# Two sides of one memory: a pool of matmul operands moved from the upper to the lower end of the partitions, the stage pools from the lower to the upper

## The chip, the core and the metric

One core of a Trainium2 chip runs the whole program. The metric is the device time of one execution in microseconds (us), as the median of three runs. The profile is of one further execution of the same program.

## What is computed

Three transformer blocks over 512 tokens of width 1024, all in float32: forgetting attention (`fox`), dilated attention in three groups (`dil`), each followed by a gated embedding layer (`ple`), and a second block with a short convolution, sparse attention in three branches and a gated feed-forward layer. Cut to what matters here, the reference is a chain of projections:

```python
h = h + fox_mixer(rms_norm(h, fox_norm[j]), fox_w_in[j], fox_b_f[j], fox_w_out[j])
h = h + (p[i] @ ple_w_up[i]) * jax.nn.sigmoid(h @ ple_w_gate[i])      # after each mixer
h = h + dilated_mixer(rms_norm(h, dil_norm[j]), dil_w_in[j], dil_w_out[j])
...
proj = h @ w_in[l]
mix = gm[..., :D_MODEL] * (y_a @ w_a_out[l]) + gm[..., D_MODEL:] * (y_b @ w_b_out[l])
x = x + mix @ w_o[l]
gu = h @ w_ffn_in[l]
x = x + (jax.nn.silu(g) * gu[..., D_FF:]) @ w_ffn_out[l]
```

## The kernel before

Every projection is a product of a weight and an activation that are each split into a high and a low fp32r part, so one product takes three matmuls: high by high, high by low, low by high (`mm3`, L144 to L146). The activation of a layer stands in SBUF as eight pairs of tiles of 128 partitions by 512 tokens, 2048 bytes in each partition: `a0h, a0l, ... a7l` (pool `x`, called A) and `b0h, b0l, ... b7l` (pool `xb`, called B). A layer reads one of the two and writes the other:

- `fo` (8 units) reads B; gate 0 (8) reads A; `dq`, `dk`, `dz` (56) and `dv` (24) read B; `do` (8) reads A; gate 1 (8) reads B.
- In the second block most units read A; `wa` and `wb` (4 each) read one half of B; `wo` (8) and the feed-forward's `fg` and `fu` (44) read half their tiles from A and half from B; `f2` (22) takes its tiles in turn, four from B and four from A.

A unit is one weight of 128 by 1024 floats: a 512 KB DMA, a copy on ACT for the high part (`whi`, L74), a subtraction on DVE for the low part (`wlo`, L85), and 24 matmuls of 512 columns. In most units (`t_unit`, `k_outer`, `t_two`) the weight is the stationary operand and A or B moves; in `n_chunk` (L248 to L250: `v`, `dv`, `nq`, `nkv`) the weight moves and 128 columns of A or B are stationary. For two of the three groups of `dv` those 128 columns are every fourth one.

The order of the work is written out by hand; nothing schedules it. Units are woven with the steps of the attention of the stage. Waits follow from the tiles: a tile that is placed where an earlier one lay waits for the last access to the earlier one.

SBUF is handed out from both ends of a partition. From the lower end: `const`, `small`, the weights (`w`), A (`x`), and on top of them the pool of the stage that runs (`fox`, `ple0`, `dil`, `ple1`, `b2` with `b2t`, `b2a`, `b2g`, `wo`, `ffn`), which is opened when the stage begins and closed at its end. From the upper end: B alone (`open_b`, `side="right"`). While `b2t` lives, B is closed. The start of some tiles, in bytes within a partition, and what is left over multiples of 64:

| tiles | before | left over 64 | changed | left over 64 |
|---|---|---|---|---|
| A: `a0h` (16 tiles, 2048 apart) | 78016 | 0 | 77824 | 0 |
| B: `b0h` (16 tiles, 2048 apart) | 196576 | 32 | 110592 | 0 |
| weights: `whi`, `wlo` (first of five) | 37056, 57536 | 0 | 36864, 57344 | 0 |
| `fox`: `v_sb` | 110784 | 0 | 147360 | 32 |
| `fox`: `qs`, `kk`, `pr`, `pt` (first) | 148192, 156384, 164576, 177120 | 32 | 184768, 192960, 201152, 213696 | 0 |
| `ple0`, `ple1`: `p0h` | 147648, 147648 | 0 | 212672, 211104 | 0, 32 |
| `ple0`: `hA` | 110784 | 0 | 175808 | 0 |
| `dil`: `dqk`, `dpt` | 140480, 175552 | 0 | 185792, 220864 | 0 |
| `b2`: `q00`, `k00h` | 110784, 127168 | 0 | 178944, 195328 | 0 |
| `b2t`: `qn`, `kd` | 160864, 212800 | 32, 0 | 122912, 174848 | 32, 0 |
| `b2a`: `pr`, `pt` | 160864, 173536 | 32 | 144768, 157440 | 0 |
| `small`: `nacc` | 18432 | 0 | 18336 | 32 |

Of the kernel before, what the change touches and what calls it, by code (L numbers as in the profile page):

```python
# [9 lines left out]
F32 = mybir.dt.float32  # L10
# [6 lines left out]
P = 128  # L17
S = 512
D = 1024
KT = 8  # L20
# [86 lines left out]
def run(chunks):  # L107
    for c in chunks:
        if c:
            c()  # L110
# [17 lines left out]
class Net:  # L128
# [19 lines left out]
    def t_unit(self, tag, pair, kts, evac, m=P, tag_ps="acc"):  # L148
# [7 lines left out]
        for u, lst in enumerate(kts):  # L156
            for c0 in range(0, len(lst), 4):
                sub = lst[c0 : c0 + 4]

                def chunk(u=u, sub=sub, c0=c0, first=(c0 == 0), pos=pos):  # L160
                    if pos == 0:
                        st["acc"] = self.bank(tag_ps)
                    if first:
                        st["w"] = self.w.pop(tag)
                    self.w.pump()
                    wh, wl = st["w"]
                    for j, (c, k) in enumerate(sub):
                        self.mm3(st["acc"][:m], wh[:, c : c + m], wl[:, c : c + m], *pair[k],
                                 pos + j == 0, pos + j == total - 1)
                    if c0 + len(sub) == len(kts[u]):  # L170
                        self.w.n_done += 1
                    if pos + len(sub) == total:
                        self.soft_end()
                        run([evac(st["acc"])])

                chunks.append(chunk)
                pos += len(sub)
# [5 lines left out]
    def k_outer(self, tags, evacs, pair):  # L183

        st = {}

        def chunk(k):
            if k == 0:
                st["w"] = [self.w.pop(t) for t in tags]
                st["a"] = [self.acc() for _ in tags]  # L190
            self.w.pump()
            for (wh, wl), a in zip(st["w"], st["a"]):
                self.mm3(a, wh[:, k * P : (k + 1) * P], wl[:, k * P : (k + 1) * P], *pair[k],
                         k == 0, k == KT - 1)
            if k == KT - 1:
                self.w.n_done += len(tags)

        def evac():
            rest = [e(a) for e, a in zip(evacs, st["a"])]
            self.w.finish()  # L200
            run(rest)

        return [lambda k=k: chunk(k) for k in range(KT)] + [evac]
# [57 lines left out]
    def rsqrt(self, y, t, a):  # L261
        run(self.rsqrt_steps(y, t, a))
# [42 lines left out]

    def norm_factors(self, ss, n):

        r = self.small.tile([P, 3, 8], F32, name="rr", tag="rr", bufs=1)
        t, a, y = r[:, 0, :n], r[:, 1, :n], r[:, 2, :n]
        self.nc.vector.tensor_scalar(t, ss[:, :n], 1.0 / D, EPS, ALU.mult, ALU.add)  # L310
        self.rsqrt(y, t, a)
        return y
# [75 lines left out]
    def run(self):  # L388
        ctx, tc, nc, t = self.ctx, self.tc, self.nc, self.t
        pool = lambda name, bufs=1, **k: ctx.enter_context(tc.tile_pool(name=name, bufs=bufs, **k))  # L390
        c = pool("const")
        self.small = pool("small")
        wpool = pool("w")
        xp = pool("x")
        self.ps = pool("ps", space=bass.MemoryType.PSUM)
        self.w = Weights(tc, wpool, self.plan(), raw_ahead=7, ahead=4, raw_bufs=3, bufs=5)

        self.ident = c.tile([P, P], F32, name="ident")
        self.ones = c.tile([P, 1], F32, name="ones")
        self.sel = c.tile([P, 32], F32, name="sel")  # L400
        nc.vector.memset(self.ones, 1.0)
        self.gains = c.tile([P, 6, KT], F32, name="gains")
        nc.sync.dma_start(self.gains[:, 0:5, :], t["gains"])
        self.pos = c.tile([P, 4], I32, name="pos")
        self.sin, self.cos = (c.tile([P, 4, 32], F32, name=n) for n in ("sin", "cos"))
        self.inv = self.sin[:, 0, :]

        self.A = self.eight(xp, "a")
        self.open_b()
        self.h_dram = tc.dram_tile([D, S], F32, name="h_dram")  # L410
        self.m1_dram = tc.dram_tile([D, S], F32, name="m1_dram")
        self.x2_dram = tc.dram_tile([D, S], F32, name="x2_dram")
        self.fox()
        self.ple(0)
        self.dil()
        if self.stop == "dil":
            self.ples.close()
            return
        self.ple(1)
        self.block2()  # L420
        if self.stop == "b2":
            return
        self.ffn()
        self.bs.close()
# [3 lines left out]

    def open_b(self):
        self.bs = ExitStack()  # L430
        bp = self.bs.enter_context(self.tc.tile_pool(name="xb", bufs=1, side="right", reuse_waits="tile"))
        self.B = self.eight(bp, "b")


    def fox(self):
        tc, nc, t = self.tc, self.nc, self.t
        es = ExitStack()
        at = es.enter_context(tc.tile_pool(name="fox", bufs=1, reuse_waits="tile"))
        A, B = self.A, self.B
        v_sb = at.tile([P, 4, D], F32, name="v_sb")  # L440
        xs = v_sb.rearrange("p a (b s) -> p (a b) s", b=2)
# [261 lines left out]
    def ple_open(self, res_src, i):  # L703
        nc = self.nc
        self.ples = ExitStack()
        self.pl = self.ples.enter_context(self.tc.tile_pool(name=f"ple{i}", bufs=1, reuse_waits="tile"))
        self.hA = self.pl.tile([P, KT, S], F32, name="hA")
        self.u = self.pl.tile([P, KT, S], F32, name="u")
        for n in range(KT):
            nc.sync.dma_start(self.hA[:, n, :], self.rows(res_src, n))  # L710
        pr = self.pl.tile([P, 2, S], F32, name="p_raw")
        self.pp = [tuple(self.pl.tile([P, S], F32R, name=f"p{k}{x}") for x in "hl") for k in range(2)]
        for k in range(2):
            nc.sync.dma_start(pr[:, k, :], self.t["pT"][i, k * P : (k + 1) * P, :])
        self.pr = pr
# [49 lines left out]
    def dil(self):  # L765
        tc, nc, t = self.tc, self.nc, self.t
        es = ExitStack()
        at = es.enter_context(tc.tile_pool(name="dil", bufs=1, reuse_waits="tile"))
        A, B = self.A, self.B
        dist = self.load(at, "dist", t["dil_dist"], 1, (P, 1280))  # L770
        v = [at.tile([P, 4, S], F32, name=f"v{g}") for g in range(3)]
# [173 lines left out]
    def block2(self):  # L945
        tc, nc, t = self.tc, self.nc, self.t
        self.bs.close()
        es, es2 = ExitStack(), ExitStack()
        at = es.enter_context(tc.tile_pool(name="b2", bufs=1, reuse_waits="tile"))
        tmp = es2.enter_context(tc.tile_pool(name="b2t", bufs=1, reuse_waits="tile"))  # L950
        A = self.A
        v = nc.vector
        R = {}
# [7 lines left out]
        mwin = self.load(at, "mwin", t["mwin"], 1)  # L961
        mcmp = self.load(at, "mcmp", t["mcmp"], 1, (P, 132))
        cw = self.load(at, "cw", t["cw"], 1, (P, 12))
        rope = []
        self.ng = self.load(at, "ng", t["b_ng"].broadcast_to([P, 256]), 1, (P, 256))
        qn = tmp.tile([P, 4, S], F32, name="qn")
# [345 lines left out]
        es2.close()  # L1312
        self.open_b()
        es3 = ExitStack()
        aa = es3.enter_context(tc.tile_pool(name="b2a", bufs=1, reuse_waits="tile"))
        rest = conv[self.PRE :]
        for i in range(4):
            rest += T("g1", ev_gm(2 * i, 0)) + T("g1", ev_gm(2 * i + 1, 0))
# [5 lines left out]
        run(rest[: self.SK])  # L1324
        weave(rest[self.SK :], [lambda j=j: slot(j) for j in range(48 + LAG + 2)])
        es3.close()
        bb = es.enter_context(tc.tile_pool(name="b2g", bufs=1, reuse_waits="tile"))
        for n in range(3):
            fetch_m1(n)
        run(g2[0] + g2[1] + wb[0] + g2[2] + g2[3] + wb[1] + g2[4] + g2[5] + g2[6] + g2[7] + wb[2] + wb[3])  # L1330
        es.close()
        wo = ExitStack()
        wp = wo.enter_context(tc.tile_pool(name="wo", bufs=1, reuse_waits="tile"))
        hr = {}
        self.norm_begin()

# [47 lines left out]
    def ffn(self):  # L1384
        tc, nc, t = self.tc, self.nc, self.t
        v = nc.vector
        es = ExitStack()
        at = es.enter_context(tc.tile_pool(name="ffn", bufs=1, reuse_waits="tile"))
        cw = self.load(at, "fcw", t["fcw"], 1, (P, 88))
        act = at.tile([P, 22, S], F32, name="act")  # L1390
        cv = [at.tile([P, 514], F32, name=f"fcv{i}") for i in range(3)]
# [47 lines left out]
        for k in range(22):  # L1439
# [3 lines left out]
            if k < 22 - last:  # L1443
                wh, wl = self.w.pop("f2")
                for n in range(KT):
                    if n == 4:
                        self.w.pump()
                    c = n * P
# [5 lines left out]
        for n in range(KT):  # L1454
            for k, (wh, wl) in held:
                c = n * P
# [118 lines left out]
```

## Time and profile before

| | us |
|---|---|
| runs | 1758.46, 1757.23, 1757.28 (median 1757.28) |
| the profiled execution's own time | 1755.62 |
| its span, first to last instruction | 1753.8 |
| PE busy in the span | 1737.2 |
| DVE, ACT, POOL busy | 967.3, 673.4, 111.5 |

The span is 1.8 us shorter than its execution's own time, and that time is 1.7 us below the median of the runs. In the rows further down, a line such as L144 is a line of the kernel before; PE is the matrix engine, PEld its loading of the stationary operand, which runs beside it. A matmul's duration goes from its start to its end; since matmuls overlap in the engine, the step from one start to the next is what a matmul costs.

### The profile page before, as it was taken

How to read it: one execution, taken by the hardware profiler on the slowest of the kernel's cores; microseconds unless marked ns; L12 is line 12 of the kernel's file. 1: busy time of each engine (PE TensorE's matmuls, PEld its weight loads, DVE VectorE, ACT ScalarE, POOL GpSimd, SP SyncE). 2: the span in 40 equal slices, each digit the busy share in tenths (PEclk: the TensorE clock that was granted, in tenths of full speed). 3: DMA queues.
4: the chain of work that ended last, by engine and by line, in shares of the span. 5: the costliest groups of instructions: out<-in, count | busy, mean ns of one | idle time of the engine just before them, and what ended most of it. 6: DMA issues, size and time to landing. Idle time of an engine off the chain costs nothing.

```text
span 1753.8 us, 21614 instructions
## 1 busy us (share of the span) xinstructions
PE 1737.2 (99%) x8512; PEld 1400.6 (80%) x8512; DVE 967.3 (55%) x1692; ACT 673.4 (38%) x1146; POOL 111.5 (6%) x88
## 2 busy tenths in 40 slices
PE   8999999999999999999999999999999999999999
PEld 6777777888977779977778786777788888888887
DVE  6477774542354443354455777776544675566332
ACT  5466653422222222222245445455432333333220
POOL 2000000100000000000000411000000122111000
PEclk9999999999999999999999999999999999999999
DMA  5422224323222223222233422112233433223421
GB/s 165 143 87 96 84 68 144 125 103 113 84 85 70 75 72 96 84 84 70 75 107 121 158 95 72 58 51 92 87 130 118 151 121 96 93 91 100 139 96 59
DMA packets 57351, 173.75 MB, mean 99 GB/s; under 512 B 7441, under 2 KB 7953, under 8 KB 57249
## 3 DMA queue, kind: packets, MB, share of 16 engines
q1 hardware_dynamic: 57248, 172.36, 29.8%
q8 instruction: 67, 1.10, 0.3%
q14 instruction: 36, 0.29, 0.1%
HBM read 161.82 MB, written 10.52 MB: 98 GB/s over the span
## 4 chain that ended last, share of the span: by engine, by line
PE 93%; DVE 4%; ACT 2%; POOL 1%; issue 0%; DMA 0%; SPq 0%; ACTq 0%; DVEq 0%
PE acc L144 21%; PE acc L146 20%; PE acc L145 20%; PE acc L248 3%; PE acc L250 3%; PE acc L249 3%; PE o L698 2%; PE t L690 2%; PE s L144 1%; PE s L146 1%; PE s L145 1%; PE s L248 1%; PE s L250 1%; PE s L249 1%; PE s L677 1%; PE s L676 1%
## 5 line engine op out<-in xcount | busy, mean ns | idle before, releaser
L85 DVE TENSOR_TENSOR wlo<-wraw,whi 128x1024 fp32r<-128x1024 f32 x267 | 347.9, 1309 | 139.1 <-ACT whi L74 138.9
L74 ACT ACTIVATE whi<-wraw 128x1024 fp32r<-128x1024 f32 x267 | 279.2, 1050 | 166.3 <-PE acc L145 71.4
L626 ACT ACTIVATE pr<-pr,st 128x512 f32<-128x512 f32 (+3 forms) x160 | 93.6, 586 | 155.7 <-DVE st L823 83.9
L291 POOL TENSOR_TENSOR nacc<-nacc,sq 128x512 f32<-128x512 f32 x35 | 47.9, 1378 | 1198.2 <-ACT sq L290 1197.8
L779 DVE TENSOR_TENSOR dqk<-acc,nacc 128x512 f32<-128x512 f32 x24 | 26.1, 1100 | 63.7 <-PE s L812 59.0
L693 ACT ACTIVATE pt<-t 128x512 f32<-128x512 f32 (+3 forms) x128 | 51.0, 424 | 18.8 <-PE t L690 17.8
L1410 ACT ACTIVATE fy<-fcv,fcw 128x512 f32<-128x512 f32 x22 | 18.0, 816 | 102.6 <-DVE fcv L1405 102.6
L1423 POOL TENSOR_TENSOR act<-fs,fu 128x512 f32<-128x512 f32 x22 | 43.8, 1991 | 195.6 <-DVE fu L1422 178.1
L690 PE MATMUL t<-ident,pr 128*128 128x128 f32 x320 | 51.0, 273 | 2.2 <-ACT pt L693 1.2
L690 PEld LDWEIGHTS t<-ident,pr 128*128 128x128 f32 x320 | 39.7, 139 | 14.4 <-DVE pr L638 1.6
L144 PE MATMUL acc<-a0h,whi 128*128 128x512 f32 x112 | 48.5, 433 | 1.2 <-DVE zh L609 1.2
L822 DVE SCALAR_TENSOR_TENSOR pr<-dist,s 128x128 f32<-128x128 f32 (+1 forms) x96 | 24.9, 315 | 44.3 <-PE s L816 44.3
L144 PE MATMUL acc<-b4h,whi 128*128 128x512 f32 x113 | 46.5, 411 | 0.0
L635 DVE RECIPROCAL st<-st 128x1 f32<-128x1 f32 x160 | 24.1, 158 | 40.5 <-ACT pr L626 40.5
L144 PE MATMUL acc<-b7h,whi 128*128 128x512 f32 x113 | 45.5, 403 | 0.0
L145 PE MATMUL acc<-b7l,whi 128*128 128x512 f32 x113 | 45.3, 401 | 0.0
L146 PE MATMUL acc<-b7h,wlo 128*128 128x512 f32 x113 | 45.2, 400 | 0.0
L144 PE MATMUL acc<-b5h,whi 128*128 128x512 f32 x113 | 44.9, 397 | 0.0
L145 PE MATMUL acc<-b6l,whi 128*128 128x512 f32 x113 | 44.7, 396 | 0.0
L146 PE MATMUL acc<-b4h,wlo 128*128 128x512 f32 x113 | 44.7, 396 | 0.0
L146 PE MATMUL acc<-b5h,wlo 128*128 128x512 f32 x113 | 44.7, 395 | 0.0
L144 PE MATMUL acc<-b6h,whi 128*128 128x512 f32 x113 | 44.6, 395 | 0.0
(1107 smaller groups left out, 4694.6 us busy)
## 6 DMA issues: line engine op xcount, KB each, us to landing
wraw<-in_dil_q SPq DMA_DIRECT2D x24, 512.0 KB, 3.3
wraw<-in_dil_k SPq DMA_DIRECT2D x24, 512.0 KB, 3.3
wraw<-in_dil_v SPq DMA_DIRECT2D x24, 512.0 KB, 3.3
wraw<-in_f_g SPq DMA_DIRECT2D x22, 512.0 KB, 3.5
wraw<-in_f_u SPq DMA_DIRECT2D x22, 512.0 KB, 3.6
wraw<-in_f_o SPq DMA_DIRECT2D x22, 512.0 KB, 3.5
wraw<-in_gate SPq DMA_DIRECT2D x16, 512.0 KB, 3.3
wraw<-in_b_gm SPq DMA_DIRECT2D x16, 512.0 KB, 3.5
```

What stands on the lines that cost most here:

```text
L74: nc.scalar.activation(hi, t, AF.Copy)
L85: self.nc.vector.tensor_tensor(lo, t, hi.bitcast(F32), ALU.subtract)
L144: mm(acc, wh, xh, start=start, stop=False)
L145: mm(acc, wh, xl, start=False, stop=False)
L146: mm(acc, wl, xh, start=False, stop=stop)
L248: self.nc.tensor.matmul(a, sh, mh, start=(k == 0), stop=False)
L249: self.nc.tensor.matmul(a, sh, ml, start=False, stop=False)
L250: self.nc.tensor.matmul(a, sl, mh, start=False, stop=(k == KT - 1))
L291: nc.gpsimd.tensor_tensor(self.nacc[i], self.nacc[i], sq, ALU.add)
L626: self.nc.scalar.activation(pr, pr, AF.Exp, scale=-1.0, bias=st[:, 0:1], accum_out=st[:, 1:2])
L690: nc.tensor.transpose(tp[:, c : c + P], pr[:, c0 + kb * P : c0 + (kb + 1) * P], self.ident)
L693: nc.scalar.activation(pts[h][:, self.KOFF[kb] : self.KOFF[kb] + b - a], tp[:, a:b], AF.Copy)
```

## The change

The stage pools take the upper end of the partitions and B the lower, right above A. `gains` and `rr` move from `const` and `small` to a new pool `edge` at the very top, and two unused tiles (`align`, 96 bytes in each partition; `align2`, 32 bytes) fill up `const` and `b2`. No instruction is added, taken away or put elsewhere in any engine's order; what differs is where tiles lie, and with it which earlier tile some instructions wait for.

```diff
@@ norm_factors
-        r = self.small.tile([P, 3, 8], F32, name="rr", tag="rr", bufs=1)
+        r = self.edge.tile([P, 3, 8], F32, name="rr", tag="rr", bufs=1)
@@ run
         xp = pool("x")
+        self.edge = pool("edge", side="right")
...
-        self.gains = c.tile([P, 6, KT], F32, name="gains")
+        c.tile([P, 24], F32, name="align")
+        self.gains = self.edge.tile([P, 6, KT], F32, name="gains")
@@ open_b
-        bp = self.bs.enter_context(self.tc.tile_pool(name="xb", bufs=1, side="right", reuse_waits="tile"))
+        bp = self.bs.enter_context(self.tc.tile_pool(name="xb", bufs=1, reuse_waits="tile"))
@@ fox; the same in ple_open, dil, block2 (b2, b2t, b2a, b2g, wo) and ffn
-        at = es.enter_context(tc.tile_pool(name="fox", bufs=1, reuse_waits="tile"))
+        at = es.enter_context(tc.tile_pool(name="fox", bufs=1, side="right", reuse_waits="tile"))
@@ block2
         cw = self.load(at, "cw", t["cw"], 1, (P, 12))
+        at.tile([P, 8], F32, name="align2")
```

One place where waits differ is the opening of `ple0` behind `fox`. SyncE's queue there before (`hA` is the residual, `p_raw` the layer's embedding, `wraw` a raw weight; in brackets the engines and DMA queues that a row waits for):

```order
L44 DMA wraw<-in_fox_o 128x1024 [waits DMAHW6_49,DMAHW2_49,DVE_49]
L710 DMA hA<-in_xT 128x512 [waits PE_49]
L710 DMA hA<-in_xT 128x512 [waits DMAHW4_49]
L710 DMA hA<-in_xT 128x512 x2
L710 DMA hA<-in_xT 128x512 [waits DMAHW7_49]
L710 DMA hA<-in_xT 128x512 [waits DMAHW0_49]
L710 DMA hA<-in_xT 128x512 [waits DMAHW1_49]
L710 DMA hA<-in_xT 128x512 [waits DMAHW2_49]
L714 DMA p_raw<-in_pT 128x512 [waits DMAHW3_49,DVE_49]
L714 DMA p_raw<-in_pT 128x512 [waits DMAHW4_49]
L44 DMA wraw<-in_up 128x1024 [waits DMAHW5_49,DVE_49]
```

and with the change (two lines further down in the file):

```order
L44 DMA wraw<-in_fox_o 128x1024 [waits DMAHW6_49,DMAHW2_49,DVE_49]
L712 DMA hA<-in_xT 128x512 [waits DVE_49,PE_49]
L712 DMA hA<-in_xT 128x512 [waits DMAHW4_49]
L712 DMA hA<-in_xT 128x512 x2
L712 DMA hA<-in_xT 128x512 [waits DMAHW7_49]
L712 DMA hA<-in_xT 128x512 [waits DMAHW0_49]
L712 DMA hA<-in_xT 128x512 [waits DMAHW1_49]
L712 DMA hA<-in_xT 128x512 [waits DMAHW2_49]
L716 DMA p_raw<-in_pT 128x512 [waits DMAHW3_49,PE_49]
L716 DMA p_raw<-in_pT 128x512 [waits DMAHW4_49]
L44 DMA wraw<-in_up 128x1024 [waits DMAHW5_49,DVE_49]
```

The first load of `hA` now lies where `fox` kept small operands that DVE reads last, and waits for DVE beside PE; before, it lay on `v_sb`, which PE reads last. At the opening of `dil`, in the same way, the load of `dist` no longer waits for the writes of `hA` to DRAM, and the first `dqk` on DVE does.

## Rows read from the trace of the kernel before

**Rows 1.** The page's parts 1 and 4: busy time of the engines, and the chain of work that ended last.

```profile
PE 1737.2 (99%) x8512; PEld 1400.6 (80%) x8512; DVE 967.3 (55%) x1692; ACT 673.4 (38%) x1146; POOL 111.5 (6%) x88
...
PE 93%; DVE 4%; ACT 2%; POOL 1%; issue 0%; DMA 0%; SPq 0%; ACTq 0%; DVEq 0%
```

**Rows 2.** Busy time by stretch: for PE, PEld, DVE, ACT and POOL the us and the instructions, then TensorE's granted clock as a share of full speed, the DMA share and GB/s. The last stretch is the start of `dil`.

```profile
1500.00:1600.00 100.00, 100.00 (x433) 81.02 (x432) 64.51 (x70) 34.77 (x43) 16.08 (x9) 1.00 0.29 91
322.00:362.00 40.00, 40.00 (x177) 33.04 (x177) 26.50 (x30) 20.74 (x31) 7.79 (x6) 1.00 0.40 138
375.90:379.40 3.50, 3.50 (x9) 2.73 (x10) 1.84 (x11) 1.06 (x1) 0.00 (x0) 0.52 0.00 0
```

**Rows 3.** ACT's rows of gate 0, which reads A, in order of time: start, duration, then the instruction and what it waited for. One `th` follows the end of each unit of 24 matmuls.

```profile
320.66 0.60 ACT L748 ACTIVATE th<-acc 128x512 f32<-128x512 f32 x1 [3.89 <-PE acc L146]
326.10 0.60 ACT L748 ACTIVATE th<-acc 128x512 f32<-128x512 f32 x1 [1.16 <-PE acc L146]
...
358.74 0.60 ACT L748 ACTIVATE th<-acc 128x512 f32<-128x512 f32 x1 [1.16 <-PE acc L146]
```

**Rows 4.** The same of gate 1, which reads B.

```profile
951.75 0.60 ACT L748 ACTIVATE th<-acc 128x512 f32<-128x512 f32 x1 [0.93 <-PE acc L146]
957.35 0.60 ACT L748 ACTIVATE th<-acc 128x512 f32<-128x512 f32 x1 [0.71 <-PE acc L146]
962.95 0.60 ACT L748 ACTIVATE th<-acc 128x512 f32<-128x512 f32 x1 [0.70 <-PE acc L146]
968.55 0.60 ACT L748 ACTIVATE th<-acc 128x512 f32<-128x512 f32 x1
974.89 0.58 ACT L748 ACTIVATE th<-acc 128x512 f32<-128x512 f32 x1
```

**Rows 5.** PE's rows of one stretch of the feed-forward layer, in order of time: start, duration, matmul. One unit is 12 matmuls on A and 12 on B.

```profile
1500.21 0.40 PE L144 MATMUL acc<-a0h,whi 128*128 128x512 f32 x1
...
1501.83 0.39 PE L145 MATMUL acc<-a2l,whi 128*128 128x512 f32 x1
...
1502.74 0.39 PE L146 MATMUL acc<-a3h,wlo 128*128 128x512 f32 x1
1502.96 0.40 PE L144 MATMUL acc<-b4h,whi 128*128 128x512 f32 x1
...
1505.77 0.40 PE L144 MATMUL acc<-a0h,whi 128*128 128x512 f32 x1
```

**Rows 6.** Instructions by tile: duration in ns (least, median, most), first and last start in us. The first two have the tile moving in a layer's product, the others (with PEld, the load) stationary in `dv` (B) and in the two projections on A.

```profile
L144 PE MATMUL acc<-p0h,whi x16: 389/389/392, 304.1 to 944.6; 128*128 128x512 f32 x16
...
L144 PE MATMUL acc<-b5h,whi x113: 393/397/502, 269.7 to 1626.0; 128*128 128x512 f32 x113
...
L249 PE MATMUL acc<-wlo,b0h x18: 396/397/403, 397.6 to 708.7; 128*128 128x512 f32 x18
...
L249 PE MATMUL acc<-wlo,b1h x18: 392/399/409, 398.3 to 709.4; 128*128 128x512 f32 x18
...
L249 PE MATMUL acc<-wlo,a1h x9: 389/389/389, 56.9 to 1031.9; 128*128 128x512 f32 x9
```

**Rows 7.** DVE in the feed-forward layer, in order of time: the first evacuation of each pair of units.

```profile
1500.41 0.69 DVE L1405 TENSOR_TENSOR fcv<-acc,rb 128x512 f32<-128x512 f32 x1 [3.28 <-PE acc L146]
...
1511.53 0.69 DVE L1405 TENSOR_TENSOR fcv<-acc,rb 128x512 f32<-128x512 f32 x1 [3.28 <-PE acc L146]
```

**Rows 8.** DVE at the program's end, in order of time: an evacuation after each 15 matmuls of `f2` (9 on B, 6 on A).

```profile
1746.69 0.69 DVE L1458 TENSOR_TENSOR fr<-fr,acc 128x512 f32<-128x512 f32 x1 [2.80 <-PE acc L146]
1750.17 0.69 DVE L1458 TENSOR_TENSOR fr<-fr,acc 128x512 f32<-128x512 f32 x1 [2.79 <-PE acc L146]
```

**Rows 9.** PE at two places of the second block's scores, in order of time: matmuls of 512, 384 and 128 columns on a moving operand that starts at a multiple of 64 bytes.

```profile
1087.34 0.39 PE L676 MATMUL s<-k00h,q 128*128 128x512 f32 x1
1087.57 0.39 PE L677 MATMUL s<-k00l,q 128*128 128x512 f32 x1
...
1090.52 0.33 PE L676 MATMUL s<-k00h,q 128*128 128x384 f32 x1
1090.69 0.34 PE L677 MATMUL s<-k00l,q 128*128 128x384 f32 x1
1090.86 0.22 PE L676 MATMUL s<-k00h,q 128*128 128x128 f32 x1
1090.92 0.27 PE L677 MATMUL s<-k00l,q 128*128 128x128 f32 x1
```

**Rows 10.** The chain of work that ended last, in gate 1, in order of time: start, us, what (one turn of a loop through ACT and DVE).

```profile
967.67 0.96 ACT whi L74
968.66 2.15 DVE wlo L85
970.81 0.61 DVE th L749
971.45 0.70 DVE hA L750
972.17 0.72 ACT a3h L330
972.90 1.14 ACT sq L290 x2
974.04 0.96 ACT whi L74
```

**Rows 11.** The end of `fox` and the opening of `ple0`, in order of time; with the issue of a DMA on SyncE's queue (SPq) the duration is that of issuing.

```profile
269.82 4.38 SPq L710 DMA_DIRECT2D hA<-in_xT  x8
269.83 0.69 DVE L550 TENSOR_TENSOR zh<-o,zs 128x512 f32<-128x512 f32 x1 [7.81 <-PE o L698]
...
271.22 0.69 DVE L328 TENSOR_TENSOR b7l<-zh,b7h 128x512 fp32r<-128x512 f32 x1 [0.70 <-ACT b7h L327]
...
274.92 0.69 DVE L718 TENSOR_TENSOR hA<-hA,acc 128x512 f32<-128x512 f32 x1 [3.01 <-PE acc L146]
```

**Rows 12.** The page's part 6: DMA issues, count, KB each, median us to landing.

```profile
wraw<-in_dil_q SPq DMA_DIRECT2D x24, 512.0 KB, 3.3
...
hA<-in_xT SPq DMA_DIRECT2D x8, 256.0 KB, 4.0
```

**Rows 13.** Stationary loads of two tiles of `b2t`, by tile: duration in ns (least, median, most), first and last start in us.

```profile
L1064 PEld LDWEIGHTS t<-ident,kd x8: 138/140/142, 1068.1 to 1077.9; 128*128 128x128 f32 x8
...
L1054 PEld LDWEIGHTS t<-ident,qn x16: 137/139/143, 1049.4 to 1074.0; 128*128 128x128 f32 x16
```

More of the change, by code (lines that the diff above doesn't have):

```diff
@@ L705, in ple_open @@
         self.ples = ExitStack()
-        self.pl = self.ples.enter_context(self.tc.tile_pool(name=f"ple{i}", bufs=1, reuse_waits="tile"))
+        self.pl = self.ples.enter_context(self.tc.tile_pool(name=f"ple{i}", bufs=1, side="right", reuse_waits="tile"))
         self.hA = self.pl.tile([P, KT, S], F32, name="hA")
@@ L767, in dil @@
         es = ExitStack()
-        at = es.enter_context(tc.tile_pool(name="dil", bufs=1, reuse_waits="tile"))
+        at = es.enter_context(tc.tile_pool(name="dil", bufs=1, side="right", reuse_waits="tile"))
         A, B = self.A, self.B
@@ L948, in block2 @@
         es, es2 = ExitStack(), ExitStack()
-        at = es.enter_context(tc.tile_pool(name="b2", bufs=1, reuse_waits="tile"))
-        tmp = es2.enter_context(tc.tile_pool(name="b2t", bufs=1, reuse_waits="tile"))
+        at = es.enter_context(tc.tile_pool(name="b2", bufs=1, side="right", reuse_waits="tile"))
+        tmp = es2.enter_context(tc.tile_pool(name="b2t", bufs=1, side="right", reuse_waits="tile"))
         A = self.A
@@ L1314, in block2 @@
         es3 = ExitStack()
-        aa = es3.enter_context(tc.tile_pool(name="b2a", bufs=1, reuse_waits="tile"))
+        aa = es3.enter_context(tc.tile_pool(name="b2a", bufs=1, side="right", reuse_waits="tile"))
         rest = conv[self.PRE :]
@@ L1326, in block2 @@
         es3.close()
-        bb = es.enter_context(tc.tile_pool(name="b2g", bufs=1, reuse_waits="tile"))
+        bb = es.enter_context(tc.tile_pool(name="b2g", bufs=1, side="right", reuse_waits="tile"))
         for n in range(3):
@@ L1332, in block2 @@
         wo = ExitStack()
-        wp = wo.enter_context(tc.tile_pool(name="wo", bufs=1, reuse_waits="tile"))
+        wp = wo.enter_context(tc.tile_pool(name="wo", bufs=1, side="right", reuse_waits="tile"))
         hr = {}
@@ L1387, in ffn @@
         es = ExitStack()
-        at = es.enter_context(tc.tile_pool(name="ffn", bufs=1, reuse_waits="tile"))
+        at = es.enter_context(tc.tile_pool(name="ffn", bufs=1, side="right", reuse_waits="tile"))
         cw = self.load(at, "fcw", t["fcw"], 1, (P, 88))
```

## The prediction, made before the change was run

> **What bounds the kernel now.** I read the page's busy times and its chain first: PE is busy for 1737.2 of 1753.8 us and holds 93% of the chain [rows 1], DVE is the next at 55%. [...] So what a matmul costs from one start to the next is nearly all of the time, and a change that moves no instruction can only act through that step, or through waits.
>
> Next I compared that step between A and B. Gate 0 and gate 1 run the same code, eight units of 24 matmuls of 512 columns with the weight stationary; gate 0 moves A, gate 1 moves B. After gate 0's units `th` comes every 5.44 us (seven units from 320.66 to 358.74 [rows 3]), that is 226.7 ns a matmul. In gate 1 the first three steps are 5.60 us [rows 4], 233.3 ns a matmul. In both, `th` follows PE directly. The durations agree: 389 ns for `p0h`, which like A starts at a multiple of 64 bytes, and 397 for `b5h`, which starts 32 past one [rows 6]. Inside one unit of the feed-forward layer, with the same weight and the same PSUM tile, the step changes with the operand: the last five on A take 1.13 us (1501.83 to 1502.96, 226 ns each), the twelve on B 2.81 us (1502.96 to 1505.77, 234 ns each) [rows 5]. After B the first seven on A take 1.62 us (1500.21 to 1501.83, 231 ns) [rows 5], so a return from B to A costs some 35 ns more. A unit of both therefore takes 5.56 us (two take 11.12 from 1500.41 to 1511.53 [rows 7]) where one of A alone takes 5.44.
>
> What sets B apart in the table of tile starts is its 32 bytes over a multiple of 64 and its place above 196576. On a multiple of 64 the step goes with the columns alone: 0.23 us for 512, 0.17 for 384, 0.06 for 128 [rows 9], all near 0.444 ns a column. So no start cost per instruction is left there, and the 6.7 ns of B are something added per instruction. I take the offset as its cause.
>
> **The change part by part.** With the change B starts at a multiple of 64, as A and the weights still do. The counts are units from the list of layers, 24 matmuls each, at 24 x 6.67 ns = 0.16 us.
> - Units wholly on B, bound by PE: `fo` 8, `dil`'s `dq`, `dk`, `dz` 56, `wa` and `wb` 8, and two of gate 1: 74 x 0.16 = **11.8 us**. Gate 1's other six count nothing: from the third on a loop of ACT and DVE (`whi`, `wlo` 2.15 us, `th`, `hA`, `a3h`, two squares) takes 6.37 us a turn (967.67 to 974.04 [rows 10]), `th` then comes 6.34 us apart [rows 4], and PE waits for it.
> - Units half on B: `wo` 8, `fg` and `fu` 44: 52 x (5.56 - 5.44) = **6.2 us**.
> - `f2`: nine blocks of 24 on B before the last five are held back, 1.4 us; then eight outputs of 15 matmuls, 3.48 us apart [rows 8] against 15 x 0.2267 = 3.40, another 0.7: **2.1 us**.
> - `dv` has B stationary: 24 units. The 8 in plain order have 397 to 399 ns against 389 on A [rows 6] and I give them the same 0.16: **1.3 us**. The 16 that take every fourth column reach 409 [rows 6]; the stride can cost something of its own. Bounds: nothing, and the whole difference of about 10 ns (399 to 389) x 384 = 3.8 us; I take the 6.67 ns that the other B operands show, the nearest row: **2.6 us**.
> - Tiles that lose their multiple of 64: `ple1`'s `p` pairs, 48 matmuls x 6.67 ns = **-0.3 us**. `v_sb` loses it as the stationary operand of 128 matmuls while `pt`, which moves there, gains it; bounds -0.9 and +0.9 us, taken 0. `pr`, `qs` and `kk` gain it too: no row prices them alone, 0 to +1 us, taken 0. `nacc` is read by PE some 50 times for a norm: under 0.4 us, taken 0.
> - Waits at the openings. `hA`'s first load is issued at 269.82 now, waiting for PE [rows 11]. With the change it waits for DVE, `zh` ending at 270.52 or at the latest `b7l` at 271.91 [rows 11]: 0.7 to 2.1 us later. Behind it on SyncE's queue stand the other `hA` rows, `p_raw` and the weights of `up`. The first sum on `hA` starts at 274.92 [rows 11], a load takes 4.0 us to land [rows 12], so DVE may start up to 1 us late; but PE goes on into the units of n = 3 and needs the first PSUM tile back only 5.6 us later, which covers it. Were that cover gone, PE would lose the 2.1 us. The other openings I cost at nothing for the same reason: the loads are issued a unit or more ahead of use. Bounds 0 and 2.1 us.
> [...]
>
> Sum: 11.8 + 6.2 + 2.1 + 1.3 + 2.6 - 0.3 = **23.7 us less**. The profiled execution of 1755.62 us would be 1731.9 and its span 1730.1; its time is 1.7 us below the median of the runs, 1757.28, which becomes **1733.6**.
>
> [...]
>
> **The rivals.**
> - *The upper end is slow, not the offset.* B is also what lies highest, and no row has a full-rate operand up there on a multiple of 64. Then B still gains 23.7 us, but the stage operands that now lie above 196576 pay: by the code's loops 160 + 128 on `fox`'s `pr` and `pt`, 64 on its `kk`, 128 on `b2`'s `k`, in `dil` 120 on `pr`, 176 on `dpt` and half of 576 on `dqk`, 96 on the `p` pairs, in all 1160 matmuls x 6.67 ns = 7.7 us: 1757.3 - 23.7 + 7.7 = **1741.3**. Against it: `kd` at 212800, a multiple of 64, loads in 140 ns, and `qn` at 160864, 32 over, in 139 [rows 13], so height alone shows nothing there, if only for a stationary tile at half rate. Chance 0.07.
> - *The address is not the cause*, so nothing changes: **1757.3**. For it stands only that two layers differ in more than address; against it the switch inside one unit [rows 5]. Chance 0.05. [...]
> - *Slower: the openings wait.* Seven stages begin with loads (`ple0`, `dil`, `ple1`, `b2`, `b2g`, `wo`, `ffn`), and at the upper end their first tiles now lie on the previous stage's last-used ones. If each opening exposed one load to landing, 4.0 us [rows 12], that is 28 us: 1757.3 - 23.7 + 28 = **1761.6**. It decides from 23.7 + 3.5 = 27.2 us, 3.9 us at every one of the seven. Against it: the one place looked at in detail moves by 2.1 us at most, and some waits get shorter, as that of `dist`. Chance 0.04.
>
> **How the numbers follow.** The forecast has 0.84. Its own range: low if the strided `dv` gives all of its 3.8 us and `pr`, `pt` and the clock bring up to 2.5 more, 1730; high if strided `dv` gives nothing, an opening loses 2.1 and `v_sb` 0.9, 1739. To hold 8 in 10 I go from 1729.5 to 1741.5, which takes in the first rival. A measurement of this kernel can tell about 0.2%, 3.5 us. Faster by more: forecast and first rival, 0.91. Within it: 0.05. Slower: 0.04.
>
> **What the new profile would show.** Gate 1's first steps of `th` at 5.44 us instead of 5.60, its later ones still near 6.37; `b5h` at 389 ns; a pair of feed-forward units 10.88 us apart; the last outputs 3.40 us apart. The strided `dv` matmuls decide between 0 and 3.8 us. If `b` rows drop but `k00h`, `dpt` or `pt` rows get longer, the first rival holds. If `b` rows stay at 397, the second. New idle time of PE ended by a DMA at a stage's start would be the third.

## The result and the profile after

| | before | changed |
|---|---|---|
| runs, us | 1755.37, 1757.23, 1757.28, 1758.46 | 1738.31, 1740.25, 1740.27, 1740.29 |
| median | 1757.26 | 1740.26 |
| profiled execution, its span | 1755.62, 1753.8 | 1738.31, 1736.5 |

The ratio is 0.9903, 95% interval 0.9891 to 0.9916: 17.0 us less on the medians, 17.3 between the two profiled executions. The forecast was 1733.6 us with a range of 1729.5 to 1741.5: the sign and the range held, the sum of 23.7 us was 6 to 7 too large, and, as the experiments show, the cause was misnamed.

The page's parts 1 and 4 of the changed kernel, against [rows 1]: PE lost 18.5 us of busy time, and no other engine's changed by more than 1.0.

```profile
PE 1718.7 (99%) x8512; PEld 1401.6 (81%) x8512; DVE 967.3 (56%) x1692; ACT 672.8 (39%) x1146; POOL 111.0 (6%) x88
...
PE 92%; DVE 4%; ACT 2%; POOL 1%; issue 0%; DMA 0%; SPq 0%; ACTq 0%; DVEq 0%
```

ACT's `th` rows of gate 0 (first and last of eight) and gate 1, in order of time: start, duration, instruction, what it waited for.

```profile
320.50 0.60 ACT L750 ACTIVATE th<-acc 128x512 f32<-128x512 f32 x1 [3.92 <-PE acc L146]
...
358.58 0.60 ACT L750 ACTIVATE th<-acc 128x512 f32<-128x512 f32 x1 [1.16 <-PE acc L146]
...
942.47 0.60 ACT L750 ACTIVATE th<-acc 128x512 f32<-128x512 f32 x1 [0.81 <-PE acc L146]
947.91 0.60 ACT L750 ACTIVATE th<-acc 128x512 f32<-128x512 f32 x1 [0.55 <-PE acc L146]
953.35 0.60 ACT L750 ACTIVATE th<-acc 128x512 f32<-128x512 f32 x1 [0.54 <-PE acc L146]
959.09 0.57 ACT L750 ACTIVATE th<-acc 128x512 f32<-128x512 f32 x1
965.45 0.57 ACT L750 ACTIVATE th<-acc 128x512 f32<-128x512 f32 x1
```

Gate 0 stays at 5.44 us a unit [rows 3]. Gate 1 on B, 5.60 us before [rows 4], now also takes 5.44; a turn of 5.74 follows, and from 959.09 on ACT and DVE set 6.36 us a turn, as before.

PE in the feed-forward layer, in order of time (start, duration, matmul), to be held against [rows 5]:

```profile
1485.23 0.39 PE L144 MATMUL acc<-b4h,whi 128*128 128x512 f32 x1
...
1487.95 0.39 PE L144 MATMUL acc<-a0h,whi 128*128 128x512 f32 x1
...
1489.54 0.39 PE L145 MATMUL acc<-a2l,whi 128*128 128x512 f32 x1
```

Twelve on B take 2.72 us (226.7 ns each; 234 before), and the seven on A after them 1.59 (227; 231 before). DVE's first evacuation of each pair of units, against [rows 7], and the last two outputs of `f2`, against [rows 8]:

```profile
1488.15 0.69 DVE L1408 TENSOR_TENSOR fcv<-acc,rb 128x512 f32<-128x512 f32 x1 [3.03 <-PE acc L146]
...
1499.04 0.69 DVE L1408 TENSOR_TENSOR fcv<-acc,rb 128x512 f32<-128x512 f32 x1 [3.03 <-PE acc L146]
1509.91 0.69 DVE L1408 TENSOR_TENSOR fcv<-acc,rb 128x512 f32<-128x512 f32 x1 [3.03 <-PE acc L146]
...
1729.55 0.69 DVE L1461 TENSOR_TENSOR fr<-fr,acc 128x512 f32<-128x512 f32 x1 [2.71 <-PE acc L146]
1732.95 0.69 DVE L1461 TENSOR_TENSOR fr<-fr,acc 128x512 f32<-128x512 f32 x1 [2.71 <-PE acc L146]
```

10.88 us a pair and 3.40 an output, as the prediction said. Instructions by tile (least, median, most ns), against [rows 6]:

```profile
L144 PE MATMUL acc<-b5h,whi x113: 389/389/499, 270.2 to 1611.0; 128*128 128x512 f32 x113
...
L144 PE MATMUL acc<-p0h,whi x16: 392/394/400, 303.6 to 935.4; 128*128 128x512 f32 x16
...
L249 PEld LDWEIGHTS acc<-wlo,b0h x18: 187/308/310, 396.4 to 701.9; 128*128 128x128 f32 x18
L249 PE MATMUL acc<-wlo,b0h x18: 389/394/395, 396.6 to 702.2; 128*128 128x512 f32 x18
```

Two rows don't fit the prediction. `p0h` rose from 389 to 394 ns in both layers, though in `ple0` it still starts at a multiple of 64. And the strided `dv` (`wlo,b0h`, whose load of every fourth column takes 308 ns against 187 for a plain one) stays at 394, not 389.

The opening of `ple0` in order of time, against [rows 11]: the load of `hA` is issued 2.6 us later, right behind `b7l` (ends at 272.38), and the first sum on `hA` starts at 275.28 instead of 274.92. That is 0.36 later, no more than the 0.47 by which `zh`, ahead of all this, had come later already: the cover that the prediction named held.

```profile
271.69 0.69 DVE L328 TENSOR_TENSOR b7l<-zh,b7h 128x512 fp32r<-128x512 f32 x1 [0.70 <-ACT b7h L327]
272.46 3.66 SPq L712 DMA_DIRECT2D hA<-in_xT  x8
...
275.28 0.69 DVE L720 TENSOR_TENSOR hA<-hA,acc 128x512 f32<-128x512 f32 x1 [2.90 <-PE acc L146]
```

Two windows of the granted clock (columns as in [rows 2]): the start of `dil`, where before it read 0.52 for 3.5 us, and the second block's attention, where before it read 1.00. Each holds two levels, so that its value is a mean: 0.50 from 377 to 379 us and from 1107 to 1109, 1.00 from 374.9 to 375.9 and from 1110 to 1111.

```profile
374.90:379.90 5.00, 5.00 (x16) 4.06 (x17) 1.84 (x11) 1.06 (x1) 0.00 (x0) 0.66 0.00 0
1105.00:1111.00 6.00, 5.59 (x21) 4.35 (x20) 4.27 (x16) 4.63 (x14) 0.00 (x0) 0.72 0.00 0
```

### The profile page after: what moved, and what is told of

Same layout as the page of the kernel before. It is cut to its first block, busy times and chain, and to the rows that moved or that the text cites. A ratio compares the mean times of both kernels' runs of the same rounds, so it can differ in the third digit from the quotient of the medians.

```text
span 1736.5 us, 21611 instructions
## 1 busy us (share of the span) xinstructions
PE 1718.7 (99%) x8512; PEld 1401.6 (81%) x8512; DVE 967.3 (56%) x1692; ACT 672.8 (39%) x1146; POOL 111.0 (6%) x88
## 4 chain that ended last, share of the span: by engine, by line
PE 92%; DVE 4%; ACT 2%; POOL 1%; issue 0%; DMA 0%; SPq 0%; ACTq 0%; DVEq 0%
PE acc L144 21%; PE acc L146 20%; PE acc L145 20%; PE acc L248 3%; PE acc L250 3%; PE acc L249 3%; PE o L700 2%; PE t L692 2%; PE s L144 1%; PE s L145 1%; PE s L146 1%; DVE wlo L85 1%; PE s L248 1%; PE s L679 1%; PE s L250 1%; PE s L249 1%
## 5 line engine op out<-in xcount | busy, mean ns | idle before, releaser
L146 PE MATMUL acc<-a0h,wlo 128*128 128x512 f32 x112 | 44.3, 395 | 0.0
L145 PE MATMUL acc<-a0l,whi 128*128 128x512 f32 x112 | 44.1, 394 | 0.0
L145 PE MATMUL acc<-a1l,whi 128*128 128x512 f32 x112 | 43.9, 392 | 0.2 <-DVE a1l L331 0.2
L145 PE MATMUL acc<-b4l,whi 128*128 128x512 f32 x113 | 44.1, 390 | 0.0
(1107 smaller groups left out, 4686.5 us busy)
```

What stands on the lines that cost most here:

```text
L145: mm(acc, wh, xl, start=False, stop=False)
L146: mm(acc, wl, xh, start=False, stop=stop)
```

## The experiments

B differed from A in three things at once: its 32 bytes over a multiple of 64 (theory O), its height (theory H, the first rival), and, which the prediction had not seen, its distance from the weights. Before, A, `p`, `whi` and `wlo` all start 192 bytes past a multiple of 256, and B 224 past one. With the change A, B and the weights start on multiples of 256, while the `p` tiles are 192 and 160 past one: of the tiles that move in a projection they alone left the weights, and they became slower. That is theory R: what counts is the moving tile's start less the stationary one's, modulo 256 bytes.

**1. B at the lower end, but 32 bytes on.** The changed kernel with a pad:

```diff
@@ open_b (changed kernel)
+        bp.tile([P, 8], F32, name="off")
         self.B = self.eight(bp, "b")
```

> B stays at the lower end, 32 bytes higher (b0h 110624, 32 over a multiple of 64). Theory O: B's step is 233 ns again, and the kernel 17 to 20 us longer than with the change, 1757 to 1760 us. Theory R: the same, since the weights do not move. Theory H: no change against the changed kernel, 1740 us, B at 227 ns.

Median 1756.93 us, against before 1.0004 (0.9994 to 1.0014): the whole gain is gone with 32 bytes. Gate 1 (`th` rows of ACT) is at 5.60 again. H is out.

```profile
953.83 0.60 ACT L751 ACTIVATE th<-acc 128x512 f32<-128x512 f32 x1 [0.93 <-PE acc L146]
959.43 0.60 ACT L751 ACTIVATE th<-acc 128x512 f32<-128x512 f32 x1 [0.71 <-PE acc L146]
```

**2. B alone, at the upper end, 32 bytes lower.** The kernel before with the same line as in 1, put behind B's tiles; as B's pool ends at the top, the pad moves B down to 196544, 192 past a multiple of 256 like the weights.

> The kernel before with B alone moved 32 bytes down, still at the upper end (b0h 196544, a multiple of 64, 64 over a multiple of 128 as whi and A). Theory O: B's step is 227 ns, time 1735 to 1740 us (below the changed kernel by what fox's attention, the p tiles and a dip of the clock cost there, 0 to 4 us). Theory R with 128: the same. Theory H: 1757 us, B at 233 ns.

Median 1737.35 us, 0.9892 (0.9877 to 0.9907): as good as the changed kernel. For the gain it does not matter at which end of the partitions B lies; 32 bytes do it.

**3. B alone, 96 bytes lower.** As in 2 with `[P, 24]`: B at 196480, a multiple of 128, and 64 bytes short of the weights' remainder.

> As the one before, but B 96 bytes down (b0h 196480, a multiple of 128, where whi and A are 64 over one). Theory O: B at 227 ns, 1735 to 1740 us, as with 32 bytes. Theory R: B differs from the weights by 64, as the p tiles of ple0 do in the changed kernel, and is slow, 233 ns, 1757 us. Theory H: 1757 us.

Median 1756.27 us, 0.9997 (0.9988 to 1.0007). B is on a multiple of 64 and of 128 and still slow; gate 1:

```profile
951.78 0.60 ACT L749 ACTIVATE th<-acc 128x512 f32<-128x512 f32 x1 [0.93 <-PE acc L146]
957.38 0.60 ACT L749 ACTIVATE th<-acc 128x512 f32<-128x512 f32 x1 [0.71 <-PE acc L146]
```

So theory O, the prediction's cause, falls; R alone said this of all three.

**4. The weights moved, A and B not.** The kernel before with

```diff
+        wpool.tile([P, 8], F32, name="off_w")
         self.w = Weights(...)
...
+        xp.tile([P, 56], F32, name="off_x")
         self.A = self.eight(xp, "a")
```

> The kernel before with the weights moved 32 bytes up and nothing else moved over multiples of 256 (A 192 past one as before, B 224 as before, whi and wlo now 224 instead of 192). Theory R (the moving tile's start less that of the weights, modulo 256, sets the step): the two layers swap their steps: gate 1 on B, which did not move, 5.44 us a unit, gate 0 on A, which did not move either, about 5.60; B's 2832 and A's 2544 matmuls with moving tiles nearly cancel, so the time is within 4 us of before, 1752 to 1760 us. Theory O (own start over 64): nothing changes, gate 0 5.44, gate 1 5.60, 1756 us.

The first pad moves the weights up by 32 bytes, the second fills A's move up to 256. One run: 1757.17 us. The two layers swapped their steps, with neither A's nor B's start changed modulo 256: gate 0 at 5.60, gate 1 at 5.44.

```profile
324.60 0.60 ACT L750 ACTIVATE th<-acc 128x512 f32<-128x512 f32 x1 [4.05 <-PE acc L146]
330.20 0.60 ACT L750 ACTIVATE th<-acc 128x512 f32<-128x512 f32 x1 [1.33 <-PE acc L146]
...
948.88 0.60 ACT L750 ACTIVATE th<-acc 128x512 f32<-128x512 f32 x1 [0.80 <-PE acc L146]
954.32 0.60 ACT L750 ACTIVATE th<-acc 128x512 f32<-128x512 f32 x1 [0.55 <-PE acc L146]
```

**5. The step by itself.** A kernel of nothing but groups of matmuls on one large tile `big`:

```python
for i in range(96):
    c = sta + (i // 3 % 8) * 128                     # stationary: eight weights in turn, each three times
    m = mov + 1024 * (i // 3 % 2) + (512 if i % 3 == 1 else 0)
    nc.tensor.matmul(acc, big[:, c:c+128], big[:, m:m+512], start=(i == 0), stop=(i == 95))
```

> This kernel leaves the whole computation out: it is groups of 96 matmuls of 512 columns (fp32r, eight weights in turn, two pairs of moving tiles, as in a unit), with nothing beside them on the other engines; only the start of the moving tile and of the weights changes from group to group, and its time is not compared with anything. Theory O (a start 32 bytes over a multiple of 64 is what costs): 226.7 ns a step wherever the moving tile starts on a multiple of 64, 233.3 at 32 past one, at any height. Theory H (what lies above some 192 KiB is slow): 226.7 for every start at 76 KiB, 233.3 from 192 KiB on. Theory R (the start of the moving tile against that of the weights counts): the value changes between moving 64 past and weights 0, and moving 64 past and weights 64 past; equal shifts of both give 226.7.

PE in order of time, one row a group: start, length, the group's name (mXwY: the moving tile X and the weights Y bytes past a multiple of 256; the profile drops a number at a name's end, and the second `m32w` to `m128w` have the weights moved as far; atXk: the moving tile at X KiB).

```profile
43.59 21.92 PE L29 MATMUL m0w<-big 128*128 128x512 f32 x96
...
132.86 22.56 PE L29 MATMUL m32w<-big 128*128 128x512 f32 x96
...
221.72 22.56 PE L29 MATMUL m128w<-big 128*128 128x512 f32 x96
244.12 21.94 PE L29 MATMUL m256w<-big 128*128 128x512 f32 x96
...
309.42 133.26 PE L29 MATMUL m0w<-big 128*128 128x512 f32 x576
442.52 21.96 PE L29 MATMUL m32w<-big 128*128 128x512 f32 x96
...
507.90 21.95 PE L29 MATMUL m128w<-big 128*128 128x512 f32 x96
...
725.54 21.92 PE L29 MATMUL at208k<-big 128*128 128x512 f32 x96
...
769.06 44.55 PE L29 MATMUL at208k<-big 128*128 128x512 f32 x192
813.45 21.95 PE L29 MATMUL sta208k<-big 128*128 128x512 f32 x96
```

21.9 us is 226.7 ns a step, 22.56 is 233.3. The x576 row holds six groups in which the weights alone moved, by 16, 32, 64, 96, 128 and 256 bytes: 226.7, 233.3, 233.3, 234.2, 232.4 and 226.7 ns. With the moving tile alone 4 bytes on it is 238.3. Offset 32 is slow at 76 KiB as at 208 KiB (the x192 row holds offsets of 32 and 64 there, 233.3 and 228.9 ns); equal offsets of 32 to 128 on both sides are as fast as none (21.95 and 21.96 us a group against 21.92); 256 apart is as good as none (21.94), 128 is not (22.56). With every fourth column stationary (steps from one start to the next) the group with equal starts takes 235.0 ns, and the one with the stationary tile 32 bytes further, as `dv` had it before the change, 237.8.

**6. All offsets, and which pairs count.** The same with more groups; `mr` and `sr` below are bytes added in turn to the moving and the stationary start.

```diff
-        c = sta + (i // 3 % 8) * 128
+        c = sta + (i // 3 % 8) * 128 + sr[i % len(sr)] // 4
-        m = mov + ...
+        m = mov + ... + mr[i % len(mr)] // 4
```

> Leaves the whole computation out, groups of 96 matmuls of 512 columns as in the probe before, and its time is not compared. With moving and stationary starts changing from matmul to matmul in turn (0, 32, 128 bytes past a multiple of 256): if a matmul's own pair counts, the group whose pairs are equal is at 226.7 ns and the two others above 230; if the stream of one matmul against the load of the next one's weights counts, the group where the weights of the next equal the moving tile of this one is at 226.7 instead. Offsets of 16 to 240 bytes: all above 226.7 but 0 (and 240, as weights 16 past cost nothing). Every fourth column stationary: 235 to 238 at any offset, as in dv. Of 384, 256 and 128 columns with 32 bytes of offset: 6.7 ns more each if it is a price per matmul, less in proportion if per column.

Mean step of matmuls 40 to 87 of a group, from their starts, by the moving start less the stationary one in bytes:

| 0 | 16 | 32 | 48 | 64 | 80 | 96 | 112 | 128 | 144 | 160 | 176 | 192 | 208 | 224 | 240 |
|---|---|---|---|---|---|---|---|---|---|---|---|---|---|---|---|
| 226.7 | 231.7 | 233.3 | 233.3 | 228.9 | 231.1 | 233.3 | 231.1 | 232.4 | 233.3 | 234.3 | 231.1 | 233.3 | 234.7 | 233.3 | 226.7 |

Only 0 and 240 are free. The kernels agree: B before (32) 233.3, `p` now 233.3 in `ple0` (192) and 234.2 in `ple1` (160). Some offsets have more than one value (48 gave 230.0 in experiment 5). With every fourth column stationary, offsets in steps of 32 give 233.3 to 240.0, where 235 to 238 was expected: alignment does not bring those to 226.7. At 384 columns offsets of 0, 32 and 64 all take 173.3 ns, at 256 columns 120.0, 117.8, 117.8, at 128 columns 111.7: the expected price per matmul is missing there, so of these lengths 512 columns alone show it. Two groups more: with one moving tile in three 32 bytes on, and with one in twelve, the mean is 231.1 ns alike, so a single displaced matmul slows those behind it too. With starts 0, 32, 128 in turn, equal pairs take 232.6 ns, weights equal to the moving tile of the matmul before 228.9, of the one after 232.2. Neither simple reading (own pair, or stream against the next load) gives 226.7, so which pair counts stays open.

**7. Breaks.** Four fp32 matmuls of 128 columns before each 12, 24 or 48.

```diff
+        if every and i % every == 0:
+            for j in range(4):
+                nc.tensor.matmul(t[:, j*128:(j+1)*128], src[:, :128], src[:, 128:256], start=True, stop=True)
```

> Leaves the whole computation out: groups of 192 matmuls of 512 columns as in the two probes before, not compared in time. Four fp32 matmuls of 128 columns stand before each 12, 24 or 48 of them, as attention's steps stand between a layer's units. Theory R with settling (after a break the product needs some 10 to 16 matmuls of about 231 ns before it runs at 226.7; at an offset of 32 or 224 it is at 233.3 from the start): what alignment saves per matmul is 6.7 ns at no break, about 4.5 at 48, 3.5 at 24 and 2 to 3 at 12. Theory R without settling: 6.7 ns at any spacing, and the units on B in dil fell short for another reason. Moving or stationary starts that change from one matmul to the next by 32 bytes: above 230 in each case. Twelve at 0 and twelve at 32 bytes in turn, as in the feed-forward layer before: 231 to 232 on the mean (5.56 us a unit), more than the mean of the two alone, 230.

PE in order of time; first pieces of 24 at offset 0, then of 24 at 32, then the same with 48. The break, `t_x`, stands between the rows shown, so that a turn is the step from one start to the next; the rows of 29 and 38 are cut off by the view's end, and only their starts count:

```profile
249.30 5.72 PE L30 MATMUL e_x<-big 128*128 128x512 f32 x24
...
255.67 5.72 PE L30 MATMUL e_x<-big 128*128 128x512 f32 x24
...
300.35 5.84 PE L30 MATMUL e_x<-big 128*128 128x512 f32 x24
...
306.84 5.84 PE L30 MATMUL e_x<-big 128*128 128x512 f32 x24
...
409.54 11.16 PE L30 MATMUL e_x<-big 128*128 128x512 f32 x48
...
421.34 6.84 PE L30 MATMUL e_x<-big 128*128 128x512 f32 x29
...
457.04 11.44 PE L30 MATMUL e_x<-big 128*128 128x512 f32 x48
...
469.13 9.11 PE L30 MATMUL e_x<-big 128*128 128x512 f32 x38
```

A turn is 6.37 against 6.49 us (5.0 ns a matmul saved) at 24, and 11.80 against 12.09 (6.0) at 48; at 12 it is 3.65 against 3.69 (3.6). So each break takes back some 35 ns of what alignment gives. The aligned stream has to settle: behind the break its steps are 236, 228, 232 and 231 ns, and only then 227. That is less than was expected here. Twelve at 0 and twelve at 32 in turn take 231.7 ns on the mean, 5.56 us a unit, just the feed-forward layer's unit before. Starts that change by 32 at every matmul take 230.0 on one side alone (expected was above 230), 233.9 on both.

**8. The rest aligned.** The changed kernel with pads, so that `p`, `qs`, `kk`, `pr`, `pt`, `dqk` and `dpt` start on multiples of 256 as well:

```diff
@@ run
+        self.edge.tile([P, 48], F32, name="top")
@@ fox
+        at.tile([P, 56], F32, name="align4")
@@ ple_open
+        if i == 1:
+            self.pl.tile([P, 56], F32, name="align3")
@@ block2
-        at.tile([P, 8], F32, name="align2")
+        at.tile([P, 24], F32, name="align2")
```

> The changed kernel with three pads at the upper end, so that the p pairs of both layers and fox's, dil's small operands start on multiples of 256 as the weights do (in the changed kernel they are 192 or 160 past one). Theory R: the p pairs go back to 226.7 ns, -0.66 us over 96 matmuls; fox's attention loses the 0.8 to 0.9 us that it is longer than before with the change if its small operands are the reason, else nothing; in all 1.5 us below the changed kernel in the profiled execution at an equal clock, 1737 to 1739 us as a median. Theory O: the p pairs of the first layer, on a multiple of 64 already, stay at 233.3, no difference, 1740 us.

Median 1736.48 us (1735.22 to 1737.22), 0.9888 (0.9872 to 0.9905) against before; the forecast was 1737 to 1739. By stage, between the two profiles: `p` -0.68 us, back at 389 ns, so R again; `fox`'s attention -0.40; the second low stretch of the clock is absent, -1.60.

**9 and 10. The changed kernel and the aligned one again, on one chip.** No further edit.

> The changed kernel itself, for more executions. [...]

> The changed kernel with the pads at the upper end, a second time and on the same chip as the changed kernel. Theory R: the lowest time is 1 to 1.5 us below the lowest of the changed kernel with as many stretches at the lower clock; the median by up to 3.5 us lower, if the stretch in the second block's attention stays away as in its first profile.

Changed: 1738.24, 1738.29, 1738.66, 1739.00, ratio 0.9893 (0.9876 to 0.9909). Aligned: 1735.71, 1737.08, 1737.18, 1737.22, ratio 0.9883 (0.9869 to 0.9898). None of the changed kernel's eight times is below 1738.2, and both its profiles have the low clock at 1107 us (0.50 from 1107 to 1109 in the first); of the aligned kernel's two profiles one has it (at 1105 us) and one not, so there it is a matter of the execution. In the five microseconds from 1100 to 1105, ahead of it, PE was busy for 3.65 us in the changed kernel's first profile and for 3.28 in the aligned one with it, against 3.25 in the aligned one without it. Whether the change makes the stretch more frequent stays open. The aligned kernel's lowest time of all is 3.0 us below the changed one's, 1.6 of it that stretch; its median here is 1.35 us lower, within what a measurement can tell. The two profiles taken here have two low stretches each, and the aligned one's execution is 1.8 us shorter (1737.22 against 1739.00).

## Why the prediction came out as it did

Sums of steps from start to start, between the two profiled executions (gate 1 with PE's wait for the last `th` in `nq` behind it: its own steps lose 1.2 us, and the wait grows by 0.9):

| term | predicted, us less | measured |
|---|---|---|
| wholly on B (`fo`, `dil`, `wa`, `wb`, gate 1) | 11.8 | 9.9 |
| half on B and `f2` | 8.3 | 8.1 |
| `dv` plain | 1.3 | 0.9 |
| `dv` strided | 2.6 (0 to 3.8) | 1.05 |
| `p` | -0.3 | -0.66 |
| `fox`'s attention | 0 | -0.9 |
| clock | 0 | -1.6 |
| openings | 0 (at worst -2.1) | +0.35 at the start of `fox` (-0.30 in the second profile of the changed kernel, so of the execution), no new wait |
| sum | 23.7 | 17.1 (17.3 by the times) |

- **The cause: the step that failed.** "I take the offset as its cause" was drawn from a table that held each start over 64, and B, which was slow, was also the one that was off the weights. Experiments 3 and 4 separate the two: B on a multiple of 128 slow (gate 1 at 5.60 us a unit), A slow with its start unchanged modulo 256 (gate 0 at 5.60). That the sign came out was luck: B's move happened to close the distance to the weights as well. Where the two causes part, in `p`, the prediction was wrong: `ple0`'s tiles were not costed at all, and the term is twice its forecast.
- **The range.** The measured 1740.26 lies above the forecast's own range, 1730 to 1739, and inside the stated one only because that was stretched to take in a rival that the runs exclude. What is missing from the sum is 1.9 us on the units wholly on B, 1.6 for the clock, 1.55 on the strided `dv` and 0.9 in `fox`'s attention.
- **Wholly on B.** 6.67 ns is the gain of an undisturbed stream. `dil`'s projections are cut by attention's steps into 33 pieces, most of 36 or 48 matmuls, and gave 7.5 us of the 9.0 that 56 units make; 33 x 35 ns of experiment 7 is 1.2 of the missing 1.5. PE behind one such break, before and then changed (start, duration, matmul):

```profile
522.07 0.50 PE L144 MATMUL acc<-b0h,whi 128*128 128x512 f32 x1
522.40 0.39 PE L145 MATMUL acc<-b0l,whi 128*128 128x512 f32 x1
...
525.67 0.39 PE L144 MATMUL acc<-b5h,whi 128*128 128x512 f32 x1
```

```profile
518.71 0.50 PE L144 MATMUL acc<-b0h,whi 128*128 128x512 f32 x1
519.04 0.39 PE L145 MATMUL acc<-b0l,whi 128*128 128x512 f32 x1
...
521.58 0.39 PE L144 MATMUL acc<-b4h,whi 128*128 128x512 f32 x1
...
522.94 0.39 PE L144 MATMUL acc<-b6h,whi 128*128 128x512 f32 x1
```

  Before, the 14 steps from `b0l` on take 3.27 us, 233.6 each. Changed, the first 11 take 2.54 us, 230.9 each, and only then it runs at 227 (six in 1.36). The prediction had seen this cost, 35 ns on the return from B to A, and did not carry it to breaks.
- **Half on B, `f2`, gate 1's loop, the end.** Right to 0.2 us in sum, and each promised row came.
- **`dv`.** The strided load has a price of its own: 235.0 ns at equal starts against 237.8 before, in the probe as in the kernel (237.7 to 235.0 over 384 matmuls). The bounds held it; the value was taken from an unstrided row. In the plain ones breaks take part of the gain, 235.5 to 230.7 over 192.
- **`fox`'s attention.** Put at 0 within bounds that went 0.9 us either way, but those were for `v_sb` and `pt`, whose steps stayed as they were. It is 0.84 us longer in its matmuls on A, which had no term: 119.93 us against 119.09, in both profiles of the changed kernel alike. Those run in pieces of 12 between steps of the scores; before, the eighth to eleventh step of a piece are 227 ns on the mean, changed they are 228 to 232. With the small operands aligned 0.43 came back, and they take 119.50. The trace of experiment 1 tells more: with B alone 32 bytes higher they take 119.00, so the extra needs B's start as well, whose last tiles hold the low parts of the keys there. Which pair makes it stays open. A guess of ours, that it is the distance of the keys in `b6h` from `qs`, fails: their step rose from 230 to 239 ns with the change and stays near 239 in the aligned kernel, where both start on multiples of 256, and it is 229 in experiment 1, where they are 96 apart.
- **Clock.** The sum has no term for the clock; the forecast's range counts it, with `pr` and `pt`, in 2.5 us, an estimate of the author's that no run shows. The runs show one low stretch at the start of `dil` before and after (0.52 for 3.5 us [rows 2], and 0.50 from 377 to 379 us), and a second with the change, in the second block's attention, whose matmuls of 512 columns step by 427 ns, about twice 227; it cost 1.6 us.
- **The rivals.** "The upper end is slow" gave 1741.3, near the measured time by accident: `dpt`'s matmuls on `v` (275 ns) and `pt`'s keep their durations above 196576 (a median of 432 ns over all forms), `p` is back at 389 ns there in experiment 8, and experiments 2 and 5 exclude height (21.92 us a group at 208 KiB as at 76). The half rate of `kd` in that rival is 109 ns a step for 128 columns, against 0.06 us in [rows 9]. "The address is not the cause" is out. "The openings wait" is out: PE's list of waits shows no DMA, before or after; its longest wait is 2.3 us in both, on ACT's `cb`.

## What to carry to other kernels

When a kernel is bound by matmuls of 512 fp32r columns, look at the start of the moving tile against that of the stationary one, modulo 256 bytes, before anything larger: a pad of 32 bytes was worth 1% here (0.9892, experiment 2), and swapping the two sides of the memory was not needed for it. A pool that is moved as a whole moves some pairs together and others apart, so list the starts of both operands of every matmul, not those of the tiles that are slow. And a contrast between two layers names a cause only when one thing differs: write down everything that differs, and look for a tile that separates it (here `p`), before costing.

## What was not expected of the hardware

- The step of a 512-column matmul depends on both starts together: 226.7 ns at a difference of 0 or 240 modulo 256, 228.9 to 234.7 at the other multiples of 16, and nothing of it at 384 columns with differences of 0, 32 and 64 (173.3 each).
- The start of the weights counts by itself: with the moving tile left where it is, weights that start 32 bytes further cost 6.7 ns a matmul (experiment 5, 226.7 to 233.3). By what way it does so no run here shows.
- After a break or a change of starts an aligned stream does not run at 226.7 ns at once. Behind the breaks of experiment 7 it took five matmuls (after the first, which a break lengthens, 236, 228, 232 and 231 ns), behind the change from B to A in the feed-forward layer before seven (224 to 241 ns, 231 on the mean [rows 5]), and behind the break in `dil` twelve (335 ns for the first, then eleven of 225 to 236). A break took back about 35 ns in all (experiment 7: 0.12 us of 6.49 saved at 24, where 24 x 6.67 ns would be 0.16).
